# Plain and seven-product pairs put into two stretches per group, with the k, v, c, h pieces between the seven-product ones

## The chip, the cores and the metric

The kernel runs on one core of a Trainium2 chip. The core has TensorE (PE; its weight loads are listed apart as PEld), VectorE (DVE), ScalarE (ACT), GpSimd (POOL) and SyncE (SP, which here only issues DMAs), 16 DMA engines, an on-chip memory and eight PSUM banks into which PE writes. Each engine works through its own instructions in the order in which they were built. The metric is the device time of one execution in microseconds, lower is better.

## The reference

One decoder layer over 272 positions (16 learned meta tokens, then 256 tokens), model width 4096:

```
h = rmsnorm(x, norm_g);  p = h @ w_in                       # 4096 x 16384
q, k, v, g_attn, b_conv, c_conv, h_conv, z_conv = split(p)  # 2048 columns each
o = stick_breaking_attention(heads(q), heads(k), heads(v))  # 16 heads of 128
o = group_rmsnorm(o * silu(g_attn), attn_norm_g, 16)
y = b_conv * short_conv(c_conv * h_conv, conv_w)            # width 3, causal, per channel
y = group_rmsnorm(y * silu(z_conv), conv_norm_g, 16)
return rmsnorm(x + concat([o, y]) @ w_out, final_norm_g)    # meta tokens dropped
```

Attention is strictly causal: a weight is sigmoid(z) times the product of (1 - sigmoid(z)) over the keys between.

## The kernel before

**Pieces.** All weights are cut into pieces of 128 x 1024, numbered in the order of work: a list `pieces` sets the order on every engine. Each piece is loaded by SP (`raw`, a ring of 5), split into a rounded part `wh` (ACT, L314) and a remainder `wl` (DVE, L315), each in a ring of 6, and multiplied on PE with three matmuls per product (L347, L349, L350, or L339 to L341), so that the result has full precision. Loads are issued 8 pieces ahead of PE, splits 5 ahead.

**Groups.** The input projection works on 8 groups of two heads and two convolution channel groups. A group has 16 pairs of pieces for q, g, b, z over the 256 tokens (a pair is two chunks of 128 of the model width, pieces "A" and "B"), and 8 blocks of four "p" pieces for k, v, c and h over all positions (24 matmuls of 258 or 272 columns in each piece). A block is named (u, kind), u being 0 or 1 in the group and kind 0 to 3 for k, v, c, h.

**Plain and seven-product pairs.** A plain pair is a 2 x 2 block product: 8 products of three matmuls with 512 columns. A seven-product pair does it with 7 (Strassen's way, in Winograd's form): beside A and B it has two pieces "T" and "U" that are sums of weights, made by DVE (L324, L327, L328), and it takes ready-made sums of the activations (`sum`, tiles `S[j]`). It needs no product into `D22`; but as P1, P5, P6, P7 are summed apart, a group with both kinds has eight accumulators: D11, D12, D21, D22, P1, P5, P6, P7, one PSUM bank each. Group 0 has no seven-product pairs; groups 1 to 7 have seven of them (`SJ`), in turn with nine plain ones.

**Order of a group.** First all 16 pairs, then the eight blocks (32 p pieces). The accumulators lie in banks 0 to 7 during the pairs; the blocks and all small work then take banks 4 to 7 in turn. The group's attention and convolution stand beside its p pieces as "tasks", each put after a given piece: `q_t` (transposes of q), `scores`, `weights`, `trans` (transposes and block copies of the weights, `at`), `po` (the product with v), for u = 0 and 1, then `norm`, `mix` (transposes of the result, `mxh` and `mxc`, and its store to `mixd`), `conv_t` (`ct`) and `conv_out`.

**After the groups** come the output projection's four groups 8 to 11 (pairs again, six of seven products in each, in `OUT_ORDER`), 8 thin pieces, and the final norm. The attention of group 7 and its last `mix` still run beside the first pairs of group 8.

Of the kernel before, what the change touches and what calls it, by code (L numbers as in the profile page):

```python
# [61 lines left out]
def kernel(ctx, tc, xt, xin, xm, par, fg, w1, w2, out):  # L62
# [11 lines left out]
    turn = [0]  # L74
    hd = {}

    def bank(nm, i=None):

        if i is None:
            i = turn[0] % 8 if "all" in hd else 4 + turn[0] % 4  # L80
            turn[0] += 1
        return pp.tile([P, 512], F32, tag=f"b{i}", name=nm)
# [15 lines left out]
    pieces = []  # L98
    ends = {}
    fin = {}  # L100
    ms = [("m", g) for g in range(GROUPS - 1)]
    for g in range(GROUPS):
        for j in range(KC // 2):
            pieces += [(q, g, j) for q in ("ABTU" if seven(g, j) else "AB")]
            if g == 0 and 4 <= j < 13:
                pieces.append(("x", j - 4))
        fin[g] = len(pieces) - 1
        for u, b in ((0, 0), (0, 1), (1, 0), (1, 1), (0, 2), (0, 3), (1, 2), (1, 3)):
            for kc in range(4):
                pieces.append(("p", (2 * g + u, b), kc))  # L110
            ends.setdefault(g, []).append(len(pieces) - 1)
            if g == GROUPS - 1 and b == 2 + u:
                pieces += ms[2 * u:2 * u + 2]
    n1 = len(pieces)

    for g in range(GROUPS, GROUPS + 4):
        for at_, j in enumerate(OUT_ORDER):
# [7 lines left out]
    n = len(pieces)  # L125

# [9 lines left out]

    mixd = [dp.tile([P, 4, SEQ], F32, name=f"mixd{g}") for g in range(GROUPS - 1)]
# [61 lines left out]
    S = {j: sp.tile([P, 2, 4, P], F32R, name=f"sum{j}") for j in SJ}  # L199
    xr = {}  # L200
# [8 lines left out]
    def prep_x(j, parts=1):  # L209
# [41 lines left out]
    def load(i):  # L251
# [131 lines left out]
    def mm_in(i):  # L383
# [117 lines left out]
    def plain_block(u, b, e):  # L501
# [13 lines left out]
    def evict_sums(g):  # L515

        cq = wk.tile([P, 2, 512], F32, tag="cq", name=f"cq{g}")
        cb = wk.tile([P, 2, 512], F32, tag=f"cb{g % 2}", name=f"cb{g}")
        gr[g] = dict(cq=cq, cb=cb)
        if g == 0:  # L520
            return
        p1, p5, p7, p6 = (psum.pop((g, q)) for q in (P1, P5, P7, P6))
        A.copy(out=cq[:, 0], in_=p1)
        V.tensor_tensor(out=cb[:, 0], in0=p6, in1=cq[:, 0], op=ALU.add)
        V.tensor_tensor(out=cq[:, 1], in0=p7, in1=cb[:, 0], op=ALU.add)
        V.tensor_tensor(out=cb[:, 0], in0=p5, in1=cb[:, 0], op=ALU.subtract)
        V.tensor_tensor(out=cb[:, 1], in0=p5, in1=cq[:, 1], op=ALU.subtract)

    def evict(g):
        s = gr[g]  # L530
        for q, d in ((D11, s["cq"][:, 0]), (D21, s["cq"][:, 1]), (D12, s["cb"][:, 0]), (D22, s["cb"][:, 1])):
            if g:
                V.tensor_tensor(out=d, in0=psum.pop((g, q)), in1=d, op=ALU.add)
            else:
                A.copy(out=d, in_=psum.pop((g, q)))
        for c, q in (("cq", "h"), ("cb", "c")):
# [403 lines left out]
```

## Time and profile before

| what | value |
|---|---|
| time, median of 3 runs | 1828.2 us (1828.1 to 1828.71) |
| span of the profiled execution, first to last instruction | 1825.5 us |
| PE busy | 1806.8 us (99%) |
| weight loads (PEld) | 1638.5 us (90%) |
| DVE busy | 1378.6 us (76%), 2015 instructions |
| ACT busy | 1081.2 us (59%) |
| POOL busy | 111.4 us (6%) |
| DMA | 364.27 MB, mean 200 GB/s, queue of SP 59.1% of 16 engines |
| mean granted TensorE clock | 0.997 |

Matmuls are pipelined: a row's duration is longer than the distance to the next one's start, so what a matmul costs PE in a stream is read from the distance between starts. The same holds, by less, for DVE.

### The profile page before, as it was taken

Reading aid. Unit: us, or ns where it says so; the run is one execution under the profiler, and the core shown is the slowest. Engines: PE = TensorE matmul, PEld = TensorE weight load, DVE = VectorE, ACT = ScalarE, POOL = GpSimd, SP = SyncE. Lnnn points to the kernel's source line nnn. Section 1 sums busy time; section 2 is a strip of 40 time slices with the busy share of each in tenths; the row PEclk is TensorE's granted clock in tenths of the full one; section 3 lists DMA queues with packets and bytes.
Section 4 is the critical chain, followed back from the end, with each engine's and each line's share of the span. In section 5 each row is a group of like instructions: output and inputs, shape, how many; then the busy total and the mean of one; then the engine's idle time right before and its main releaser. Section 6 shows DMA issues by size and latency. Waiting matters only on the chain.

```text
span 1825.5 us, 29438 instructions
## 1 busy us (share of the span) xinstructions
PE 1806.8 (99%) x11103; PEld 1638.5 (90%) x11103; DVE 1378.6 (76%) x2015; ACT 1081.2 (59%) x1674; POOL 111.4 (6%) x172
## 2 busy tenths in 40 slices
PE   9999999999999999999999999999999999999997
PEld 7899889988998899889988998899889977888897
DVE  6686787678767866786678667866786768898986
ACT  6766556655665566556655665566556655555554
POOL 2210001000100010001000100010001031000000
PEclk9999999999999999999999999999999999999999
DMA  8865566446654665475446655655465576675655
GB/s 292 308 213 169 164 216 209 166 164 218 204 170 159 223 201 170 160 222 205 169 161 220 203 171 162 225 197 170 158 225 196 198 260 202 228 232 192 202 181 196
DMA packets 107999, 364.27 MB, mean 200 GB/s; under 512 B 12112, under 2 KB 17360, under 8 KB 107856
## 3 DMA queue, kind: packets, MB, share of 16 engines
q1 hardware_dynamic: 103824, 358.72, 59.1%
q10 hardware_dynamic: 4032, 3.67, 0.6%
q8 instruction: 87, 1.43, 0.3%
q14 instruction: 56, 0.46, 0.1%
HBM read 354.48 MB, written 7.86 MB: 198 GB/s over the span
## 4 chain that ended last, share of the span: by engine, by line
PE 97%; DVE 1%; ACT 1%; DMA 0%; issue 0%; SPq 0%; DVEq 0%; ACTq 0%
PE P L347 17%; PE P L350 17%; PE P L349 17%; PE mm L339 14%; PE mm L340 13%; PE mm L341 13%; DVE wl L315 1%; PE mo L763 0%; PE mo L762 0%; PE mo L761 0%; PE z L609 0%; PE po L655 0%; ACT wh L314 0%; DMA raw<-w 0%; DMA xr<-xt 0%
## 5 line engine op out<-in xcount | busy, mean ns | idle before, releaser
L314 ACT CAST wh<-raw 128x1024 fp32r<-128x1024 f32 (+3 forms) x721 | 692.8, 992 | 527.2 <-PE mm L340 203.4
L315 DVE TENSOR_TENSOR wl<-raw,wh 128x1024 fp32r<-128x1024 f32 (+3 forms) x721 | 815.1, 1157 | 245.9 <-ACT wh L314 236.4
L339 PE MATMUL mm<-xs,wh 128*128 128x258 f32 (+1 forms) x2048 | 589.2, 288 | 0.9 <-ACT wh L314 0.7
L340 PE MATMUL mm<-xs,wh 128*128 128x258 f32 (+1 forms) x2048 | 581.9, 284 | 0.0
L341 PE MATMUL mm<-xs,wl 128*128 128x258 f32 (+1 forms) x2048 | 581.8, 284 | 0.0
L339 PEld LDWEIGHTS mm<-xs,wh 128*128 128x128 f32 x2048 | 385.6, 188 | 4.1 <-ACT wh L314 0.9
L340 PEld LDWEIGHTS mm<-xs,wh 128*128 128x128 f32 x2048 | 385.7, 188 | 0.6
L341 PEld LDWEIGHTS mm<-xs,wl 128*128 128x128 f32 x2048 | 385.6, 188 | 0.0
L347 PE MATMUL P<-wh,xs 128*128 128x512 f32 x779 | 304.7, 391 | 1.9 <-ACT wh L314 1.9
L350 PE MATMUL P<-wl,xs 128*128 128x512 f32 x779 | 303.7, 390 | 0.0
L349 PE MATMUL P<-wh,xs 128*128 128x512 f32 x779 | 303.6, 390 | 0.0
L347 PEld LDWEIGHTS P<-wh,xs 128*128 128x128 f32 x779 | 146.6, 188 | 32.1 <-ACT wh L314 2.2
L350 PEld LDWEIGHTS P<-wl,xs 128*128 128x128 f32 x779 | 146.5, 188 | 31.4 <-DVE wl L315 0.6
L349 PEld LDWEIGHTS P<-wh,xs 128*128 128x128 f32 x779 | 146.7, 188 | 29.9
L350 PE MATMUL P<-wl,mixh 128*128 128x512 f32 (+1 forms) x392 | 148.3, 378 | 0.5 <-DVE wl L315 0.5
L347 PE MATMUL P<-wh,mixl 128*128 128x512 f32 (+1 forms) x392 | 148.6, 379 | 0.0
L349 PE MATMUL P<-wh,mixh 128*128 128x512 f32 (+1 forms) x392 | 148.2, 378 | 0.0
L324 DVE TENSOR_TENSOR t<-raw,raw 128x1024 f32<-128x1024 f32 (+1 forms) x73 | 87.6, 1200 | 24.6 <-DMA raw<-w 24.3
L314 ACT CAST wh<-t 128x1024 fp32r<-128x1024 f32 (+1 forms) x73 | 75.7, 1036 | 46.8 <-PE P L349 32.5
L315 DVE TENSOR_TENSOR wl<-t,wh 128x1024 fp32r<-128x1024 f32 (+1 forms) x73 | 87.6, 1200 | 4.2 <-ACT wh L314 3.4
L350 PEld LDWEIGHTS P<-wl,mixh 128*128 128x128 f32 x392 | 74.2, 189 | 13.1 <-DVE wl L315 1.4
L347 PEld LDWEIGHTS P<-wh,mixl 128*128 128x128 f32 x392 | 74.3, 190 | 12.0 <-ACT wh L314 0.3
(243 smaller groups left out, 1712.4 us busy)
## 6 DMA issues: line engine op xcount, KB each, us to landing
raw<-w SPq DMA_DIRECT2D x614, 512.0 KB, 4.0
raw<-w SPq DMA_DIRECT2D x32, 384.0 KB, 3.5
raw<-xin SPq DMA_DIRECT2D x8, 512.0 KB, 4.6
xr<-xt SPq DMA_DIRECT2D x15, 272.0 KB, 4.7
raw<-mixd SPq DMA_DIRECT2D x7, 512.0 KB, 3.3
res<-xin SPq DMA_DIRECT2D x12, 256.0 KB, 5.9
out<-res SPq DMA_DIRECT2D x4, 512.0 KB, 3.2
mixd<-mfh ACTq DMA_DIRECT2D x14, 128.0 KB, 2.1
```

Of the source, the lines that this page charges most:

```text
L314: nc.scalar.copy(out=h[:, c], in_=t[:, c])
L315: nc.vector.tensor_tensor(out=lo[:, c], in0=t[:, c], in1=h[:, c].bitcast(F32), op=ALU.subtract)
L324: nc.vector.tensor_tensor(out=s[:, :2 * hw].rearrange("p (a b) -> p a b", a=2), in0=a[:, :2 * hw].rearrange("p (a b) -> p a b", a=2), in1= ...
L339: nc.tensor.matmul(out=o, lhsT=h, rhs=x[:, 0, s:], start=k == 0, stop=False)
L340: nc.tensor.matmul(out=o, lhsT=h, rhs=x[:, 1, s:], start=False, stop=False)
L341: nc.tensor.matmul(out=o, lhsT=lo, rhs=x[:, 0, s:], start=False, stop=k == KC - 1)
L347: nc.tensor.matmul(out=o, lhsT=a[1], rhs=h, start=key not in begun, stop=False)
L349: nc.tensor.matmul(out=o, lhsT=a[0], rhs=h, start=False, stop=False)
L350: nc.tensor.matmul(out=o, lhsT=a[0], rhs=lo, start=False, stop=last)
```

## The change

Two things change in the groups' order and one in their make-up.

- Each of groups 1 to 6 has eleven seven-product pairs and five plain ones; group 7 has eight and eight; group 0 stays plain. That is 25 plain pairs turned into seven-product ones.
- A new function `in_pieces` writes the order. A group begins with its plain pairs, in turn with the last two blocks (c and h of u = 1) of the group before ("R"); the attention of the group before is planned into this stretch. Then come the seven-product pairs, each followed by two p pieces of the group's own first six blocks ("S"). Plain pairs first completes D22, whose bank is copied out (`open_rows`) and is from then on the one bank for all blocks and small work of the stretch: the blocks, the second head's `po`, `mix` and `conv_t` come after one another in it (`block_bank`, `spare`). The tasks `mix`, `conv_t`, `conv_out` and the second `norm` move into the next group's seven-product stretch (`slot`). Accumulators change sides from group to group. Group 7 ends with four blocks by themselves ("Z").
- Eleven sums of activations do not fit on the chip. Five stay (`HELD`); six (`LENT`) are made in group 0 (`late_sums`), written to DRAM (`lend`) and loaded again by each group that uses them, into a ring of two (`lent`), 512 KB each.

Less weighty: `evict` takes all accumulators but D22 at one place behind the last seven-product pair, and the first output group starts its seven-product pairs one place later (`OUT_FIRST`).

```diff
-SJ = (2, 4, 6, 8, 10, 12, 14)
+HELD = (1, 4, 7, 10, 13)
+LENT = (2, 5, 8, 11, 14, 15)
+SJ = tuple(j for pair in zip(LENT, HELD + (None,)) for j in pair if j is not None)
+LAST_SJ = SJ[:8]
...
+OUT_FIRST = (0, 1, 2, 3, 4, 8, 5, 9, 6, 10, 7, 11, 12, 13, 14, 15)
...
+    first = ((0, 0), (0, 1), (0, 2), (0, 3), (1, 0), (1, 1))
+    last = ((1, 2), (1, 3))
+    for g in range(GROUPS):
+        plain = [j for j in range(KC // 2) if not seven(g, j)]
+        left = blocks_of(g - 1, last) if g else []
+        for n, j in enumerate(plain):
+            pair(g, j)
...
+            take, left = (left[:1], left[1:]) if n < 4 else ([], left)
+            for t in take:
+                block(*t)
...
+        todo = blocks_of(g, first if g < GROUPS - 1 else ((0, 0), (0, 1), (1, 0), (1, 1)))
+        for j in sevens(g):
+            pair(g, j)
+            block(*todo.pop(0))
+        for t in todo:
+            block(*t)
...
+    def late_sums(j):
+        x = xs[j // 2][:, 2 * (j % 2):2 * (j % 2) + 2, :, META:L].bitcast(F32)
+        t = wk.tile([P, 2, SEQ], F32, tag="cb1", name=f"xt{j}")
+        nc.vector.tensor_tensor(out=t, in0=x[:, :, 0], in1=x[:, :, 1], op=ALU.add)
+        d = lent(j)
+        token_sums(d, t, j)
...
+        if p[0] == "A" and 0 < p[1] < GROUPS and p[2] in LENT and seven(*p[1:]):
+            S[p[2]] = lent(p[2])
+            nc.sync.dma_start(out=S[p[2]].bitcast(F32), in_=sumd[p[2]])
...
+    def block_bank(i):
+        kind, g = zone[i]
+        (u, b), d = pieces[i][1], 4 * (g % 2)
+        if kind == "R":
+            return 4 - d
+        if kind == "Z":
+            return d + 2 * ((2 * u + b) % 2)
+        return d + D22 if g else (4, 5, 6, 0, 1, 2)[{(0, 0): 0, (0, 1): 1, (0, 2): 2, (0, 3): 3, (1, 0): 4, (1, 1): 5}[u, b]]
...
-        for u, z in ((0, f + 6), (1, f + 15)):
-            later(z, scores, g, u)
-            later(z + 3, weights, g, u)
-            later(z + 5, trans, g, u)
-            later(z + 8, po, g, u)
-        later(f + 25, norm, g, "h")
-        later(f + 29 if g < GROUPS - 1 else n1 + 1, mix, g, "h")
...
+        for u, z in ((0, 5), (1, 12)):
+            later(after(f, z), scores, g, u)
+            later(after(f, z + 3), weights, g, u)
+            later(after(f, z + 5), trans, g, u)
+            later(after(f, z + 8), po, g, u)
...
+        later(after(f, 22), norm, g, "h")
+        later(after(f, 25) if end else slot(g + 1, 2), mix, g, "h")
+        later(after(e, 2) if end else slot(g + 1, 4), conv_t, (2 * g, 2 * g + 1))
+        later(after(e, 3) if end else slot(g + 1, 4) + 1, conv_out, g)
+        later(after(e, 5) if end else slot(g + 1, 5), norm, g, "c")
+        later(after(e, 8) if end else slot(g + 1, 6), mix, g, "c")
```

**DVE, one unit.** Before, on DVE in a group's pair stretch, the unit that repeats is one seven-product pair and one plain pair (number behind `wl` and `raw`: the piece; `t` the sum for T):

```order
L324 TENSOR_TENSOR t252_6274<-raw251_6215,raw252_6233 128x1024
L315 TENSOR_TENSOR wl250_6252<-raw250_6203,wh250_6251 128x1024
L315 TENSOR_TENSOR wl251_6262<-raw251_6215,wh251_6261 128x1024
L315 TENSOR_TENSOR wl252_6271<-raw252_6233,wh252_6270 128x512
L327 TENSOR_TENSOR raw251_6215<-raw251_6215,t252_6274 128x512
L315 TENSOR_TENSOR wl253_6287<-t252_6274,wh253_6286 128x1024
L328 TENSOR_TENSOR raw251_6215<-raw252_6233,raw251_6215 128x512
L315 TENSOR_TENSOR wl254_6299<-raw251_6215,wh254_6298 128x1024
L315 TENSOR_TENSOR wl255_6317<-raw255_6268,wh255_6316 128x1024
```

After, on DVE in the seven-product stretch of group 3, the unit is one seven-product pair (pieces 279 to 282) and two p pieces (here 278, and 283 of the next):

```order
L396 TENSOR_TENSOR t280_6664<-raw279_6580,raw280_6611 128x1024
L387 TENSOR_TENSOR wl278_6642<-raw278_6566,wh278_6641 128x1024
L387 TENSOR_TENSOR wl279_6652<-raw279_6580,wh279_6651 128x1024
L387 TENSOR_TENSOR wl280_6661<-raw280_6611,wh280_6660 128x512
L399 TENSOR_TENSOR raw279_6580<-raw279_6580,t280_6664 128x512
L387 TENSOR_TENSOR wl281_6677<-t280_6664,wh281_6676 128x1024
L400 TENSOR_TENSOR raw279_6580<-raw280_6611,raw279_6580 128x512
L387 TENSOR_TENSOR wl282_6689<-raw279_6580,wh282_6688 128x1024
L387 TENSOR_TENSOR wl283_6719<-raw283_6658,wh283_6718 128x1024
```

The nine instructions are the same in kind and order; pieces 250 and 255 of a plain pair have become p pieces, and eleven such units now follow each other.

**PE, one hand-over of a bank.** Before, on PE, the transposes `mxh` of group 2 stand inside a block, in a bank of their own:

```order
L339 MATMUL mm5_3_5840<-xs1_125,wh225_5653 128x258
L340 MATMUL mm5_3_5840<-xs1_125,wh225_5653 128x258
L341 MATMUL mm5_3_5840<-xs1_125,wl225_5654 128x258
L577 MATMUL mxh2_5865<-ident_93,cq2_4725 128x128 x4
L339 MATMUL mm5_3_5840<-xs2_126,wh226_5684 128x258
L340 MATMUL mm5_3_5840<-xs2_126,wh226_5684 128x258
```

After, on PE in group 3's seven-product stretch (`mm6_0`, the first block, has ended nine matmuls earlier):

```order
L419 MATMUL P0_3_5711<-wh268_6434,xs2_132 128x512
L421 MATMUL P0_3_5711<-wh268_6434,xs2_132 128x512
L422 MATMUL P0_3_5711<-wl268_6435,xs2_132 128x512
L674 MATMUL mxh2_6539<-ident_99,cq2_5571 128x128 x4
L419 MATMUL P5_3_6307<-wh269_6450,lent5_6352 128x512
L421 MATMUL P5_3_6307<-wh269_6450,lent5_6352 128x512
```

The transposes have moved behind the B piece (268) of the third seven-product pair and now write the bank that the block `mm6_0` used before them and `mm6_1` uses after them.

**SP.** Before, on SP, the loads of such a unit are pieces alone:

```order
L274 DMA raw255_6268<-w1 128x1024
L274 DMA raw256_6284<-w1 128x1024
L274 DMA raw257_6296<-w1 128x1024
L274 DMA raw258_6314<-w1 128x1024
L274 DMA raw261_6349<-w1 128x1024
```

After, on SP in group 3, the sum for the seventh seven-product pair goes out in front of the B piece of the fifth:

```order
L346 DMA raw277_6550<-w1 128x1024
L346 DMA raw278_6566<-w1 128x1024
L346 DMA raw279_6580<-w1 128x1024
L328 DMA lent11_6831<-sumd11_89 128x1024
L346 DMA raw280_6611<-w1 128x1024
```

Every second unit now has a fifth load; its place in the ring of two is freed by PE's last use of the sum two rounds earlier, and the load of piece 280 stands behind that wait.

More of the change, by code (lines that the diff above doesn't have):

```diff
@@ L50, in hwid, with sevens, in_pieces, pair @@
     return 384 if g == GROUPS + 3 else 512
+def sevens(g):
+    return OUT_SJ if g >= GROUPS else SJ if 0 < g < GROUPS - 1 else LAST_SJ if g else ()
 def seven(g, j):
-    return j in (OUT_SJ if g >= GROUPS else SJ if g else ())
+    return j in sevens(g)
+def in_pieces():
+    out, zone = [], []
+    def pair(g, j):
+        for q in "ABTU" if seven(g, j) else "AB":
+            out.append((q, g, j))
+    def block(u, b, kcs):
+        for kc in kcs:
+            out.append(("p", (u, b), kc))
+    def blocks_of(g, pairs):
+        return [(2 * g + u, b, kcs) for u, b in pairs for kcs in ((0, 1), (2, 3))]
+    first = ((0, 0), (0, 1), (0, 2), (0, 3), (1, 0), (1, 1))
[5 more added lines that the diff above has]
+            pair(g, j)
+            if g == 0 and 4 <= j < 13:
+                out.append(("x", j - 4))
+            take, left = (left[:1], left[1:]) if n < 4 else ([], left)
+            for t in take:
+                block(*t)
+        for t in left:
+            block(*t)
+        zone += [("R", g)] * (len(out) - len(zone))
+        todo = blocks_of(g, first if g < GROUPS - 1 else ((0, 0), (0, 1), (1, 0), (1, 1)))
[3 more added lines that the diff above has]
+        for t in todo:
+            block(*t)
+        zone += [("S", g)] * (len(out) - len(zone))
+    for i, t in enumerate(blocks_of(GROUPS - 1, ((0, 2), (0, 3), (1, 2), (1, 3)))):
+        block(*t)
+        if i in (1, 3, 5, 7):
+            out.append(("m", i // 2))
+    zone += [("Z", GROUPS - 1)] * (len(out) - len(zone))
+    return out, zone
 G0, CW0, AG0, CG0, NPAR = 0, 32, 80, 96, 112
@@ L74 @@
     turn = [0]
+    free = [[4, 5, 6, 7]]
     hd = {}
@@ L79, in bank @@
         if i is None:
-            i = turn[0] % 8 if "all" in hd else 4 + turn[0] % 4
+            i = free[0][turn[0] % len(free[0])]
             turn[0] += 1
@@ L92 @@
     nc.sync.dma_start(out=pt, in_=par)
-    pieces = []
-    ends = {}
-    fin = {}
+    pieces, zone = in_pieces()
+    ends, fin, top = {}, {}, {}
     ms = [("m", g) for g in range(GROUPS - 1)]
[L102 to L113, printed above, removed]
+    for i, p in enumerate(pieces):
+        if p[0] == "p":
+            ends[p[1]] = i
+        elif p[0] in "ABTU":
+            top[p[1]] = i
+        if p[0] == "p" and zone[i][0] == "S":
+            fin[p[1][0] // 2] = i
     n1 = len(pieces)
     for g in range(GROUPS, GROUPS + 4):
-        for at_, j in enumerate(OUT_ORDER):
+        for at_, j in enumerate(OUT_ORDER if g > GROUPS else OUT_FIRST):
             for q in "ABTU" if seven(g, j) else "AB":
@@ L125 @@
     n = len(pieces)
+    real = [i for i, p in enumerate(pieces) if p[0] in "ABTUpo"]
+    nth = {i: q for q, i in enumerate(real)}
     where, c1, c2 = {}, 0, 0
@@ L535, in evict @@
                 A.copy(out=d, in_=psum.pop((g, q)))
+        if not g:
+            A.copy(out=cb[:, 1], in_=psum.pop((g, D22)))
         for c, q in (("cq", "h"), ("cb", "c")):
@@ L810 @@
         plan_group(g)
+    for q, j in enumerate(LENT):
+        later(after(top[0], 4 * q + 2), late_sums, j)
+        later(after(top[0], 4 * q + 4), lend, j)
     tasks.sort(key=lambda t: t[0])
-    later(fin[0], finish_stats)
+    later(top[0], finish_stats)
+    plain_end = {g: max(i for i in range(n1) if pieces[i][0] == "B" and pieces[i][1] == g and not seven(*pieces[i][1:]))
+                 for g in range(GROUPS)}
     for i in range(1 - SPLITS, n):
@@ L825 @@
         p = pieces[i]
+        if "all" not in hd:
+            free[0] = spare(i)
         if i < n1:
@@ L829 @@
                 plain_block(*p[1], i)
-            if p[0] == ("U" if p[1] else "B") and p[2] == SJ[-1]:
-                evict_sums(p[1])
+            if i in plain_end.values():
+                open_rows(p[1])
+            if i in top.values():
+                evict(p[1])
                 if p[1] == GROUPS - 1:
                     open_mix(0)
-            if i in fin.values():
-                evict(pieces[i][1])
             if i == n1 - 1:
@@ L852 @@
             if "all" not in hd:
-                hd["all"], turn[0] = True, 0
+                hd["all"], turn[0], free[0] = True, 0, list(range(8))
             _, nb, kc = p
@@ L908 @@
         hw = hwid(GROUPS + c // 1024)
-        for j in OUT_ORDER:
+        for j in OUT_ORDER if c else OUT_FIRST:
             m1, m2 = w[2 * j], w[2 * j + 1]
```

93 lines of the change are left out of this document (55 added, 38 removed).

## Prediction

> **What bounds the kernel now.** I read the busy shares first, then the chain of waits.
>
> ```profile
> span 1825.5 us, 29438 instructions
> PE 1806.8 (99%) x11103; PEld 1638.5 (90%) x11103; DVE 1378.6 (76%) x2015; ACT 1081.2 (59%) x1674; POOL 111.4 (6%) x172
> PE 97%; DVE 1%; ACT 1%; DMA 0%; issue 0%; SPq 0%; DVEq 0%; ACTq 0%
> ```
>
> The chain that ended last lies on PE for 97% of the span, so the stream of matmuls sets the time, and what the change takes out of it counts in full as long as the other engines keep up. Shares are averages over stages, so next the busy times by stretch: the p stretch of group 0, and the pair stretch and the p stretch of one later group.
>
> ```profile
> core 0: us, PE busy (x) PEld busy (x) DVE busy (x) ACT busy (x) POOL busy (x), PEclk, DMA share, GB/s
> 85.00:202.00 117.00, 117.00 (x893) 113.26 (x892) 86.15 (x159) 73.28 (x127) 6.41 (x10) 1.00 0.56 188
> 383.80:461.00 77.20, 77.20 (x344) 63.92 (x343) 65.41 (x78) 45.49 (x60) 2.50 (x4) 1.00 0.63 204
> 461.00:565.60 104.60, 104.60 (x835) 102.95 (x834) 69.53 (x123) 62.73 (x115) 6.68 (x10) 1.00 0.54 177
> ```
>
> PE is busy throughout, at full granted clock. DVE is at 65.41 of 77.20 in the pair stretch and at 69.53 of 104.60 in the p stretch: mixing the two levels its load. Third, the waits of PE for other engines; the columns are total, times, longest.
>
> ```profile
> PE mxc L577 <- ACT cb L571: 2.8, 1, 2.8
> PE mm L339 <- DVE cb L527: 0.2, 1, 0.2
> ```
>
> There is next to nothing to win back from waits. The only larger one is at the end of the groups.
>
> **The change part by part.**
>
> *Fewer matmuls.* Distances between starts, from the timeline of PE:
>
> ```profile
> 399.30 0.39 PE L347 MATMUL P<-wh,xs 128*128 128x512 f32 x1
> 399.98 0.39 PE L347 MATMUL P<-wh,sum 128*128 128x512 f32 x1
> 461.02 0.29 PE L341 MATMUL mm<-xs,wl 128*128 128x272 f32 x1
> 461.39 0.28 PE L341 MATMUL mm<-xs,wl 128*128 128x272 f32 x1
> 559.42 0.28 PE L341 MATMUL mm<-xs,wl 128*128 128x258 f32 x1
> 559.54 0.39 PE L347 MATMUL P<-wh,xs 128*128 128x512 f32 x1
> ```
>
> Three matmuls of 512 columns lie between the first two rows (one row each at L347, L349, L350): 0.68 / 3 = 0.2267 us each. Three of 272 columns take 0.37, so 0.123 each. The last two rows show a p matmul followed by a pair's: 0.12 us, so changing over costs nothing, and the change does that twice per pair. A plain pair is 24 x 0.2267 = 5.44 us, a seven-product pair 21 x 0.2267 = 4.76, a p piece 24 x 0.123 = 2.96. 25 pairs lose three matmuls each: 75 x 0.2267 = **17.0 us off PE**. The p pieces are as many as before.
>
> *More work for DVE and ACT.* Here is one unit of the pair stretch on DVE, from one wait for U's cast to the next:
>
> ```profile
> 409.07 2.36 DVE L315 TENSOR_TENSOR wl<-raw,wh 128x1024 fp32r<-128x1024 f32 x2 [1.19 <-ACT wh L314]
> 411.35 1.22 DVE L324 TENSOR_TENSOR t<-raw,raw 128x1024 f32<-128x1024 f32 x1
> 412.48 2.96 DVE L315 TENSOR_TENSOR wl<-raw,wh 128x1024 fp32r<-128x1024 f32 x3
> 415.36 0.68 DVE L327 TENSOR_TENSOR raw<-raw,t 128x512 f32<-128x512 f32 x1
> 415.96 1.22 DVE L315 TENSOR_TENSOR wl<-t,wh 128x1024 fp32r<-128x1024 f32 x1
> 417.09 0.68 DVE L328 TENSOR_TENSOR raw<-raw,raw 128x512 f32<-128x512 f32 x1
> 418.97 2.36 DVE L315 TENSOR_TENSOR wl<-raw,wh 128x1024 fp32r<-128x1024 f32 x2 [1.20 <-ACT wh L314]
> ```
>
> The unit takes 418.97 - 409.07 = 9.90 us, 1.20 of it waiting. The new unit (one seven-product pair, two p pieces) has the same nine instructions, and PE needs 4.76 + 2 x 2.96 = 10.68 us for it. A stretch of eleven wants 11 x 9.90 = 108.9 us of DVE against 11 x 10.68 = 117.5 of PE. DVE has other work there:
>
> ```profile
> L461 DVE TENSOR_TENSOR kT<-mm,rstd 128x272 f32<-128x272 f32 x16 | 6.9, 431 | 0.0
> L471 DVE STREAM_TRANSPOSE yv<-vt 128x288 f32<-128x288 f32 x16 | 7.3, 457 | 7.8 <-ACT za L637 7.8
> L452 DVE COPY vv<-yv 32x64 f32<-32x64 f32 x128 | 23.8, 186 | 1.9
> L177 DVE TENSOR_SCALAR nc<-ssc 128x4 f32<-128x4 f32 x8 | 1.6, 202 | 0.2
> L314 ACT CAST wh<-raw 128x1024 fp32r<-128x1024 f32 x612 | 626.2, 1049 | 483.0 <-PE mm L340 190.8 <-DVE raw L328 172.0 <-PE P L349 56.9
> ```
>
> Two k blocks at 0.43; one v block (0.43 by its likeness to k, 0.46, 8 x 0.19); one c, one h and the reading of `po` (seven more of 0.43 as an estimate from the k row); 22 small operations of two norms at up to 0.20: about 0.9 + 2.4 + 3.0 + 4.4 = 10.7. So DVE is about level with PE (119.6 against 117.5, plus the two p pieces at the end of the stretch, 5.9 for PE and 2 x 1.18 for DVE). It can also use the 1.20 us waits for these operations, which would take up to 13 us off. And it starts ahead: the tightest ring place is free when A begins, and its next piece is wanted a unit's rest later (1.36 + 0.68 + 1.36 + 1.36 + 2.96 = 7.7), while cast and remainder take 1.05 + 1.18. **Cost taken: 0**; the cover is that lead of some 4.4 us, when another cast of 1.05 stands before it, and its loss is the first rival below. ACT gets 25 x (1.05 + 0.55) = 40 us more and is at 59%: hidden.
>
> *One bank for many.* Three times a group (before `mxh`, `ct` and `mxc`) a block ends, PE does A and B (nine matmuls, 2.04 us), and within these DVE must have read the block: one operation in front of it (1.18) and the read (0.43) fit with 0.4 to spare. The other hand-overs have twelve matmuls (2.72) or are read by ACT. The nearest row is the second wait quoted above, in which a block's first matmul waited for DVE to have read an accumulator's bank: 0.2 us, once. Ends: 0, as PE met no such wait anywhere else, and 0.7 for each, when one more 512-column DVE operation (0.68) stands ahead. With 21 of them (groups 1 to 7): 0 to 14.7 us; a gain is excluded because the change only adds such waits. I take 0.2 each, nearer that row: **+4.2**.
>
> *Moved attention.* It has now 8 p pieces and 5 plain pairs beside it. For u = 1 before:
>
> ```profile
> 508.24 0.25 PE z L608 x2
> 525.25 2.23 ACT L454 COPY at<-ya 32x96 f32<-32x96 f32 x8
> 531.91 0.22 PE po L651 x2
> ```
>
> From `z` to the last copy of the weights are 527.48 - 508.24 = 19.2 us; `po` then stood 4.4 us behind, with nothing waiting. After, between `z` and `po` stand two plain pairs, two p pieces, A and B, and the first head's `po` (ten matmuls, some 1.1): 2 x 5.44 + 2 x 2.96 + 2.04 + 1.1 = 19.9. So it fits with 0.7 to spare: **0**, ends 0 and 7 x (2 x 1.18 - 0.7) = 11.6, if two of DVE's wide operations more hold the copies back.
>
> *Sums made, stored, reloaded.* In group 0 six sums more:
>
> ```profile
> L232 POOL TENSOR_TENSOR sf<-xr 128x128 f32<-128x128 f32 x7 | 5.8, 830 | 62.0 <-ACT xr L217 36.4 <-DVE xr L215 25.6
> raw<-w SPq DMA_DIRECT2D x614, 512.0 KB, 4.0
> ```
>
> DVE has two operations of about 0.68 each for a sum, 8.2 us, against 30.9 idle in group 0's p stretch; POOL's four of at most 0.83 come to 20 at most, in a stretch where it is busy 6.41 of 117. The reloads take 40 loads of 512 KB on SP, like a piece (4.0 us to landing). A unit in the present pair stretch loads four pieces of 0.524 MB in 4.76 + 5.44 = 10.2 us, which the window has as 204 GB/s at a DMA share of 0.63; the new unit, with a sum in every second one, loads 4.5 in 10.68: 221 GB/s, a share of about 0.68. Hidden: **0**. In SP's queue the sum waits for PE's last use of its place and the B piece of that pair stands behind; half a unit of the lead covers it, else DVE's `t` comes up to 1.5 us late.
>
> *The end of the groups.* The large wait:
>
> ```profile
> 1489.55 0.39 PE L350 MATMUL P<-wl,mixh 128*128 128x512 f32 x1
> 1492.71 1.46 PE L577 MATMUL mxc<-ident,cb 128*128 128x128 f32 x4 [2.77 <-ACT cb L571]
> 1493.82 0.78 PE L347 MATMUL P<-wh,mixl 128*128 128x512 f32 x1
> 1499.04 0.40 PE L347 MATMUL P<-wh,mixl 128*128 128x512 f32 x1
> 1494.00:1500.00 6.00, 6.00 (x18) 4.71 (x18) 3.08 (x4) 1.57 (x4) 0.00 (x0) 0.59 0.80 302
> ```
>
> The last `mix` waits 2.77 us for the norm, and then twelve matmuls take 5.22 us in place of 12 x 0.2267 = 2.72, at a granted clock of 0.59: with 0.6 for slow transposes, 5.9 us in all. After the change the same chain follows the last block by about as many pairs. **0**; ends -5.9 (wait gone) and +6 (a second such wait, for `mxh`, which is put earlier against the norm).
>
> [...]
>
> Sum against the profiled execution: 1825.5 - 17.0 + 4.2 = 1812.7. The median of the runs is 1828.2, 2.7 above that span: **1815.4, said as 1815**.
>
> **The rivals.**
>
> 1. *DVE becomes the bound in the seven-product stretches* (slower). With the 10.7 us spread over eleven units and T's sum 0.9 late by the sum's load, a unit takes 9.90 + 0.97 + 0.9 = 11.77, if none of DVE's waits are filled. Over PE's 10.68 that is 12.0 a group, less the lead of 4.4: 7.6, in six groups 46. Time: 1828.2 - 17.0 + 46 = 1857. It decides from a unit of 10.68 + (4.4 + 17.0 / 6) / 11 = 11.3 us. For it speaks that sum; against it that DVE is idle 15% of the present pair stretch and that its norms fit in the waits. Chance 0.08.
> 2. *Each hand-over is late by one wide DVE operation and more*, about 1 us, when DVE's lead is used up and it takes its order literally. 21 us: 1828.2 - 17.0 + 21 = 1832. It decides from 17.0 / 21 = 0.8 us each. For it: 0.4 us of room. Against: PE's list of waits shows one such case among 64 blocks. Chance 0.11.
> 3. *The hand-overs stop PE so often that the clock falls each time.* If each cost the 0.2 us and the 2.5 us of slow matmuls seen at the end of the groups, 21 x 2.7 = 57: 1828.2 - 17.0 + 57 = 1868. Against it: 0.2 us is far from 2.8, and the three stretches shown stand at 1.00. Chance 0.03. [...]
> 4. *All is hidden and the last wait goes too*: 1828.2 - 17.0 - 5.9 = 1805. It needs the norm of group 7 to be done 2.8 us earlier against PE; nothing in the change shortens its chain. Chance 0.13.
>
> **How the numbers follow.** The forecast (1815; its own bounds 1811 with the hand-overs at 0 and 1826 with them at 14.7) has 0.65; the rivals as above. The range from 1805 to 1828 takes in rival 4 below; above, it leaves out rivals 1 and 3 and most of rival 2 (its milder part, some 0.03, lies inside): 0.19. A difference of 0.2% (3.7 us) is about what a measurement of this kernel can tell from none. Faster than 1824.5: the forecast all but 0.02 and rival 4: 0.76. Slower than 1831.9: rivals 1 and 3 and a good third of rival 2: 0.15. Between: 0.09.
>
> **What would show it.** Right: PE's instructions 75 fewer among those of 512 columns; PE waits for DVE or ACT in the new stretches together of some 4 us, at `mxh`, `ct`, `mxc`; DVE's unit at 10.7 us, with PE the engine that ends last; one wait of some 3 us around `mxc` of group 7. Wrong, and how: waits of PE for `wl` (L387) that grow along a stretch mean rival 1; waits at L674 or at a block's first matmul (L411) above 0.8 us mean rival 2; a granted clock below 1.00 inside groups 1 to 7 means rival 3; waits of `po` mean that the attention's cover of 20 us was cut too fine; PE waiting for `lent` means that the reloads are late, which the sum takes as hidden.

## The result, and the profile after

The changed kernel takes 1845.4 us (median of 4 runs, 1842.5 to 1850.7) against 1828.15 beside it (1827.6 to 1828.7): ratio 1.0096, 95% interval 1.0074 to 1.0118. It is slower by 1%; the forecast was 0.7% faster. The profiled execution took 1842.7 us. Here and below one execution of the kernel before (1977.2 us) and one of tail_late (8597.0 us) are left out, as they lie far outside all others. From its page (span; busy time by engine; the chain that ended last, by engine):

```profile
span 1840.8 us, 29653 instructions
PE 1793.8 (97%) x11028; PEld 1621.1 (88%) x11028; DVE 1502.7 (82%) x2150; ACT 1124.2 (61%) x1735; POOL 143.2 (8%) x188
PE 86%; DVE 5%; issue 3%; ACT 2%; DMA 2%; POOL 2%; SPq 0%; DVEq 0%; POOLq 0%; ACTq 0%
```

The 75 matmuls are gone (11103 to 11028) and PE is busy 13.0 us less, yet the span has grown by 15.3: PE stands still more. The chain, 97% PE before, now passes through DVE, ACT and DMA for some 9%. What PE waits for (total, times, longest), the same view as before:

```profile
PE mxc L674 <- DVE cc L575: 12.9, 6, 2.4
PE ct L762 <- DVE cy L588: 6.6, 1, 6.6
PE mxh L674 <- DVE kT L553: 5.2, 6, 1.3
PE P L419 <- ACT wh L386: 2.8, 3, 1.7
PE mxc L674 <- DVE kT L553: 2.1, 1, 2.1
PE P L422 <- DVE wl L387: 1.8, 4, 0.6
```

Three of these rows are the transposes that now share one bank with the blocks, waiting for DVE to have read a block (`kT`, `cc`) out of it; `ct` at L588 is the end of the groups. The waits for casts (`wh`) and remainders (`wl`) shown here lie at the very start and behind the groups. By stretch, the seven-product stretch of group 3 and the plain stretch behind it:

```profile
core 0: us, PE busy (x) PEld busy (x) DVE busy (x) ACT busy (x) POOL busy (x), PEclk, DMA share, GB/s
592.00:707.00 115.00, 112.37 (x730) 102.88 (x730) 98.22 (x133) 68.25 (x102) 2.54 (x5) 1.00 0.66 214
707.00:775.00 68.00, 68.00 (x439) 61.95 (x439) 54.55 (x89) 46.22 (x80) 9.97 (x9) 1.00 0.57 192
```

The plain stretch with the attention has no idle PE at all. All of this group's loss lies in its seven-product stretch.

Adding up, over PE's timeline, by how much each start lies later than the usual distance behind the matmul before it gives 24.7 us before and 56.9 after. The difference, 32.2 us, less the 17.0 of the matmuls, gives the span's 15.3 to a tenth. Of it, 24.5 stand in front of `mxh` (6.4), `mxc` (16.6) and `ct` (1.5) in groups 1 to 7, and 7.9 after 1425 us, at the end of the groups (16.9 against 9.0).

**One hand-over, row by row.** In group 5, block c of the first head ends on PE when the A piece begins; then come A, B and `mxc`:

```profile
1020.78 0.40 PE L419 MATMUL P<-wh,xs 128*128 128x512 f32 x1
1024.78 0.63 PE L674 MATMUL mxc<-ident,cb 128*128 128x128 f32 x4 [1.78 <-DVE cc L575]
```

DVE and, below it, ACT in the same microseconds:

```profile
1019.09 0.69 DVE L400 TENSOR_TENSOR raw<-raw,raw 128x512 f32<-128x512 f32 x1
1019.69 0.16 DVE L665 TENSOR_TENSOR ssc<-nc,fac 128x4 f32<-128x4 f32 x1
1020.95 1.23 DVE L387 TENSOR_TENSOR wl<-raw,wh 128x1024 fp32r<-128x1024 f32 x1 [1.11 <-ACT wh L386]
1023.07 1.22 DVE L387 TENSOR_TENSOR wl<-raw,wh 128x1024 fp32r<-128x1024 f32 x1 [0.89 <-ACT wh L386]
1024.21 0.42 DVE L575 TENSOR_TENSOR cc<-mm,rstd 128x258 f32<-128x258 f32 x1
```

```profile
1019.87 1.06 ACT L386 CAST wh<-raw 128x1024 fp32r<-128x1024 f32 x1 [5.09 <-DVE ssc L665]
1020.83 1.27 ACT L668 ACTIVATE cb<-cb,ssc 128x128 f32<-128x128 f32 x4
1022.01 1.98 ACT L386 CAST wh<-raw 128x1024 fp32r<-128x1024 f32 x2
```

The read of c takes 0.42 us, but begins 3.4 us behind the block's end: in DVE's order stand two remainders before it, each waiting for its cast on ACT. The first cast is that of the U piece. Its wait of 5.09 us is for U's sum of weights (L400, which ended at 1019.78): the view names the norm's last operation (`ssc`), which ended 0.07 later. The second cast stands behind the norm's scaling (`cb`, 1.27 us). PE needs 2.04 us for A and B, and stops. Over the groups the reads of k ahead of `mxh` begin 2.2 to 3.0 us behind their block, those of c ahead of `mxc` 3.4 to 4.1, in groups 1 to 6. Before the change DVE stood waiting for PE at about half of the reads of v and c. The groups of these reads, kernel before (L467, L483), then changed kernel (L559, L575); the last column is DVE's idle time ahead of them and what ended it:

```profile
L467 DVE TENSOR_TENSOR vt<-mm,rstd 128x272 f32<-128x272 f32 x16 | 7.0, 437 | 8.5 <-PE mm L341 8.5
L483 DVE TENSOR_TENSOR cc<-mm,rstd 128x258 f32<-128x258 f32 x16 | 6.8, 424 | 4.8 <-PE mm L341 4.8
```

```profile
L559 DVE TENSOR_TENSOR vt<-mm,rstd 128x272 f32<-128x272 f32 x16 | 7.0, 434 | 2.0 <-PE mm L413 1.9
L575 DVE TENSOR_TENSOR cc<-mm,rstd 128x258 f32<-128x258 f32 x16 | 6.5, 407 | 0.0
```

Same operation, same duration; the slack in front of it has gone.

But late reads are not new. In the kernel before, DVE had no idle time ahead of the reads of k (0.0, the row of L461 in the prediction), and in groups 1 to 6 the first c block was read 3.56 us behind its end. Here in group 2, first the start of the next block on PE, then the read:

```profile
523.18 0.28 PE L339 MATMUL mm<-xs,wh 128*128 128x258 f32 x1
526.74 0.42 DVE L483 TENSOR_TENSOR cc<-mm,rstd 128x258 f32<-128x258 f32 x1
```

PE went on without a wait, as its next block went into another bank. The changed kernel's reads of c (3.4 to 4.1 us) are hardly later; it is the next user that now wants the same bank.

**The end of the groups.** PE's wait, and DVE in the ten microseconds before it:

```profile
1489.59 0.69 PE L762 MATMUL ct<-ident,cy 128*128 128x128 f32 x2 [6.56 <-DVE cy L588]
```

```profile
1478.94 1.83 DVE L544 COPY at<-ya 32x96 f32<-32x96 f32 x8
1482.20 0.42 DVE L580 TENSOR_TENSOR cc<-mm,cc 128x258 f32<-128x258 f32 x1
1488.86 0.67 DVE L588 SCALAR_TENSOR_TENSOR cy<-cc,pt,cy 128x256 f32<-128x256 f32 x1
```

Group 7 has only 16 p pieces left at its end, so the second head's weights (`at`) and the last convolution (`cc`, `cy`) come to DVE one right behind the other, and `ct` comes before the convolution is done. Between the convolution's steps DVE has remainders and sums for the output projection to make, too.

### The profile page after: what moved, and what is told of

It is laid out like the page before. It is cut to its first block, busy times and chain, and to the rows that moved or that the text cites. A ratio compares the mean times of both kernels' runs of the same rounds, so it can differ in the third digit from the quotient of the medians.

```text
span 1840.8 us, 29653 instructions
## 1 busy us (share of the span) xinstructions
PE 1793.8 (97%) x11028; PEld 1621.1 (88%) x11028; DVE 1502.7 (82%) x2150; ACT 1124.2 (61%) x1735; POOL 143.2 (8%) x188
## 4 chain that ended last, share of the span: by engine, by line
PE 86%; DVE 5%; issue 3%; ACT 2%; DMA 2%; POOL 2%; SPq 0%; DVEq 0%; POOLq 0%; ACTq 0%
PE P L419 16%; PE P L422 16%; PE P L421 16%; PE mm L413 11%; PE mm L412 11%; PE mm L411 11%; DVE wl L387 2%; DMA raw<-w 1%; ACT wh L386 1%; DMA raw<-mixd 1%; PE mo L868 0%; PE mo L867 0%; PE mo L866 0%; PE z L706 0%; DVE raw L400 0%
## 5 line engine op out<-in xcount | busy, mean ns | idle before, releaser
L386 ACT CAST wh<-raw 128x1024 fp32r<-128x1024 f32 (+2 forms) x746 | 710.3, 980 | 499.9 <-DVE raw L400 160.8
L387 DVE TENSOR_TENSOR wl<-raw,wh 128x1024 fp32r<-128x1024 f32 (+2 forms) x746 | 837.1, 1149 | 174.9 <-ACT wh L386 171.1
L419 PE MATMUL P<-wh,xs 128*128 128x512 f32 x654 | 259.5, 397 | 1.7 <-ACT wh L386 1.7
L422 PE MATMUL P<-wl,xs 128*128 128x512 f32 x654 | 255.1, 390 | 0.3 <-DVE wl L387 0.2
L421 PE MATMUL P<-wh,xs 128*128 128x512 f32 x654 | 254.9, 390 | 0.0
L396 DVE TENSOR_TENSOR t<-raw,raw 128x1024 f32<-128x1024 f32 (+1 forms) x98 | 118.2, 1206 | 35.1 <-DMA raw<-w 33.1
L422 PEld LDWEIGHTS P<-wl,xs 128*128 128x128 f32 x654 | 122.7, 188 | 27.2 <-DVE wl L387 1.1
L419 PEld LDWEIGHTS P<-wh,xs 128*128 128x128 f32 x654 | 123.0, 188 | 24.5 <-ACT wh L386 1.9
L421 PEld LDWEIGHTS P<-wh,xs 128*128 128x128 f32 x654 | 122.9, 188 | 21.8
L386 ACT CAST wh<-t 128x1024 fp32r<-128x1024 f32 (+1 forms) x98 | 101.7, 1038 | 45.5 <-PE P L421 14.5
L387 DVE TENSOR_TENSOR wl<-t,wh 128x1024 fp32r<-128x1024 f32 (+1 forms) x98 | 117.9, 1203 | 4.8 <-ACT wh L386 4.7
```

Source lines behind the costliest of these rows:

```text
L386: nc.scalar.copy(out=h[:, c], in_=t[:, c])
L387: nc.vector.tensor_tensor(out=lo[:, c], in0=t[:, c], in1=h[:, c].bitcast(F32), op=ALU.subtract)
L396: nc.vector.tensor_tensor(out=s[:, :2 * hw].rearrange("p (a b) -> p a b", a=2), in0=a[:, :2 * hw].rearrange("p (a b) -> p a b", a=2), in1= ...
L419: nc.tensor.matmul(out=o, lhsT=a[1], rhs=h, start=key not in begun, stop=False)
L421: nc.tensor.matmul(out=o, lhsT=a[0], rhs=h, start=False, stop=False)
L422: nc.tensor.matmul(out=o, lhsT=a[0], rhs=lo, start=False, stop=last)
```

## The experiments

The theories: A, a block's read is late because of what stands ahead of it in DVE's order; B, DVE simply has more work than PE in the stretch; C, the reloaded sums hold up the queue of loads. For the end of the groups, T1 to T3. Medians stand against 1845.4 (changed) and about 1828 (before, measured beside each).

**Later transposes (t_slot).**

```diff
-        return pieces.index(("B", g, sevens(g)[c]))
+        return pieces.index(("T", g, sevens(g)[c]))
```

> The transposes mxh, ct and mxc stand behind the T piece in place of the B piece: 15 matmuls (3.4 us) instead of 9 (2.04 us) between a block's end and them, and 6 (1.36 us) instead of 12 before the next block uses the bank. Changed kernel: PE waits 5.2 us for mxh and 15.0 for mxc over seven groups, median 1845 us. Theory A (DVE reads the block 1.0 to 2.3 us too late, because the read stands in DVE's order behind remainders for pieces further ahead): the wait for mxh goes below 1 us, that for mxc to about 6 (7 x 0.9), waits at the next block for ACT below 2; about 14 us less, 1831. Theory B (DVE has more work in the stretch than PE, so PE must wait somewhere): the waits move to remainders (wl), the time stays within 4 us of 1845. Theory C (the loads of the sums hold up the pieces): as B.

Median 1834.4 us (1832.1 to 1837.0), ratio to the kernel before 1.0032 (1.002 to 1.0044). PE's waits:

```profile
PE mm L411 <- ACT cy L764: 11.8, 7, 2.6
PE ct L762 <- DVE cy L588: 6.4, 1, 6.4
PE mm L411 <- ACT mfc L685: 0.7, 4, 0.2
```

The waits for `mxh` and `mxc` are gone altogether, and no remainder is waited for instead (1.7 us in all, 2.0 in the changed kernel): against B. The other side of the hand-over was too short at one place in each group: the block behind `ct` waits for ACT, whose reading of `ct` stood behind its copies of v's blocks (2.9 us in group 5). Not foreseen, and the reason for 1834 in place of 1831.

**Without the reloads (no_lent).**

```diff
-            S[p[2]] = lent(p[2])
-            nc.sync.dma_start(out=S[p[2]].bitcast(F32), in_=sumd[p[2]])
+            S[p[2]] = S[HELD[0]]
```

> The 40 reloads of sums are left out; the pairs that used them multiply one of the resident sums instead (other numbers, the same matmuls). Theory A (DVE's order) and theory B (DVE's amount of work): nothing changes, 1845 us within 4, waits for mxh and mxc within 20% of 5.2 and 15.0 us. Theory C (the loads in SP's queue delay the B pieces, these DVE's sums, and these its reads of the blocks): both waits fall by half or more, 10 to 20 us less, 1825 to 1835.

Median 1840.9 us (1840.2 to 1846.9; the changed kernel 1842.5 to 1850.7).

```profile
PE mxc L673 <- DVE cc L574: 10.8, 6, 2.4
PE mxh L673 <- DVE kT L552: 5.1, 6, 1.0
```

`mxh` waits as before, `mxc` 12.8 in place of 15.0 (with the row of 2.0 for `kT`). The reloads cost between nothing and 5 us (4.5 at the medians, with ranges that overlap); C is not the cause.

**mxc one block later (mxc_slot8).**

```diff
-else slot(g + 1, 6), mix, g, "c")
+else slot(g + 1, 8 if g < GROUPS - 2 else 6), mix, g, "c")
```

> The transposes mxc alone stand one block later (behind the ninth seven-product pair instead of the seventh, groups 1 to 6), so that the norm on DVE and its scaling on ACT lie a block ahead of the read that they wait for. Theory A1 (of the 2.3 us at mxc some 1.3 come from the norm: its small operations on DVE and the scaling on ACT stand ahead of the casts and remainders in front of the read): the wait for mxc falls from 2.1 to 2.6 us each to about 1.0 in six groups, 8 us less, about 1837. Rival A2 (a block's read comes that late there by DVE's remainders alone): the wait stays above 1.8 us each and the time within 3 us of 1845.

Median 1851.4 us (1845.8 to 1853.6): 6 us more, though the ranges overlap. The wait has clearly grown:

```profile
PE mxc L674 <- DVE cc L580: 17.6, 6, 3.6
```

Neither theory has this: A1 expected shorter waits, A2 the same time. The read of h, now the one in front, begins 3.7 to 5.2 us behind its block (1.8 to 2.9 in the changed kernel in groups 2 to 6, where PE had stopped a block earlier). So a stop of PE ahead of the block had let DVE catch up; without it DVE is later at the next. In mxc_R below, where nothing stops PE there, h is read 3.1 to 4.3 us behind as well.

**Without the norm's operations on DVE (no_norm).** In `norm`:

```diff
-        V.tensor_scalar(out=ss, ...); r = rsqrt_raw(ss, ...); V.tensor_tensor(out=ss, ...)
+        if q == "h" or g == GROUPS - 1:
+            V.tensor_scalar(out=ss, ...); r = rsqrt_raw(ss, ...); V.tensor_tensor(out=ss, ...)
```

> In the changed kernel's order, the eleven small DVE operations of the convolution's norm are left out in groups 0 to 6 (its scaling on ACT then uses the plain sum of squares and does not wait for DVE; other numbers). The read of c, ahead of mxc, started 3.4 to 4.1 us behind its block's end; that of k, ahead of mxh, 2.2 to 3.0. Theory A1 (the norm holds DVE and ACT back by the difference, and with DVE and PE level there nothing makes it up within a block): c's read comes 2 to 2.7 us behind, the waits for mxc fall from 15.0 us to 7, and the median by 8, to 1837. Rival A2 (c's read is late by the remainders alone): both within 20%, the median within 3 us of 1845.

Median 1833.8 us (1831.1 to 1837.3), 11.6 less.

```profile
PE mxc L675 <- DVE cc L575: 6.2, 6, 1.7
PE mxh L675 <- DVE kT L553: 4.4, 6, 0.8
```

c's read comes 2.2 to 3.4 us behind, and `mxc` waits 6.5 in place of 15.0. Eleven operations of under 0.2 us, and the scaling that waits for them, make the difference between `mxh` and `mxc`. That fits A, with a share of B: DVE has so little to spare that 2 us of small work aren't made good within a block.

**Only mxh and mxc later (hc_T), `ct` behind B.**

```diff
-... slot(g + 1, 2), mix, g, "h")
-... slot(g + 1, 6), mix, g, "c")
+... slot(g + 1, 2, "T"), mix, g, "h")
+... slot(g + 1, 6, "T"), mix, g, "c")
```

> mxh and mxc alone stand behind the T piece; ct stays behind the B piece. With all three behind T, PE waited 11.8 us for ACT to read ct (seven times 1.3 to 2.6 us) and not at all for mxh and mxc; with ct behind B, the changed kernel had waited 0.9 us for it. Theory A (a read of the bank is late by what stands ahead of it in its engine's order, so each hand-over wants the longer side where the later reader is): the waits for mxh, mxc and ct together fall below 4 us, the median goes from 1834.4 (all three behind T) to about 1825, level with the kernel before or 0.2% faster. Theory B (DVE has more work than PE there): the time won shows up as waits for remainders and the median stays above 1831.

Median 1836.6 us (1833.3 to 1839.8), no better than with all three behind T.

```profile
PE mxc L674 <- DVE cc L575: 5.7, 6, 1.0
PE mm L411 <- ACT mfc L685: 5.5, 6, 0.9
```

Without the stop at `ct`, c's read is again 3.7 to 4.0 us late, more than the 3.4 that T allows; and `mxc`, late itself, leaves ACT too little time ahead of the next block. A wait taken away in this stretch came back one place on, as with mxc_slot8.

**The convolution later in group 7 (tail_late); the attention earlier (tail_early).**

```diff
# tail_late: conv_t, conv_out, norm c, mix c at e + 5, 6, 8, 11 in place of 2, 3, 5, 8
# tail_early:
-        for u, z in ((0, 5), (1, 12)):
+        for u, z in ((0, 3), (1, 9)) if end else ((0, 5), (1, 12)):
```

> Group 7 alone: its conv_t, conv_out, second norm and second mix stand three pieces later beside group 8. In the changed kernel PE waits 6.6 us there for DVE's convolution, followed by half the granted clock. Theory T1 (the convolution stands on DVE behind the weights of the second head's attention, which in group 7 have moved next to it; PE comes too early): the wait goes below 1.5 us and the slow clock behind it goes, 7 to 10 us less, about 1837. Rival T2 (DVE is 7 us behind there with all its work, so PE waits for the next remainder instead): the time stays within 3 us of 1845 and a new wait of 4 us or more stands in the next 20 us.

> Group 7 alone: both heads' attention begins two and three pieces earlier, with the convolution where it was. Putting the convolution and the second mix later had only moved the wait (from ct, 6.6 us, to mxh and mxc, 4.7 us). Theory T3 (in group 7 the weights of the second head's attention and the convolution come to DVE and ACT in the same ten microseconds; apart, neither is late): the wait at ct falls from 6.6 us below 1.5, no new one above 1.5 stands in the next 40 us, and the median falls by 6 to 9 us, to about 1837. Rival T2 (DVE and ACT are behind there by their amount of work): waits of together 4 us or more remain between group 7's last block and the end of mxh and mxc, the median above 1841.

Medians 1842.8 (1841.8 to 1844.9) and 1844.0 us (1842.0 to 1845.2): within 3 us of the changed kernel, which its own range of 8 us doesn't tell from nothing. PE's waits in the tail, first of tail_late:

```profile
PE mxc L674 <- issue: 2.4, 1, 2.4
PE mxh L674 <- ACT cq L668: 2.1, 2, 1.8
```

then of tail_early:

```profile
PE mxh L674 <- ACT cq L668: 2.3, 2, 2.0
PE ct L762 <- DVE cy L588: 0.3, 1, 0.3
```

The wait at `ct` goes either way, as T1 and T3 had it, and smaller ones come up where a norm's scaling is late: 4.5 us in two places in tail_late, where ACT scales for `mxc` only at 1514.55 us and the transposes begin at 1515, and 2.3 in tail_early. Neither brought the 6 to 10 us expected. The late starts after 1425 us fall from 16.9 to 12.6 us with the earlier attention; the time doesn't show it, since in that profile half-clock stretches behind stops at `mxc` came in four groups, where the changed kernel's profile has one (three more at 1.7 us each; see the end). One of them shows a granted clock of 0.76 from 1209 to 1216 us, and the mean over that profile is 0.993 against 0.996.

**Both together (hc_T_tail).**

> Both edits together: mxh and mxc behind T, group 7's attention earlier. Under theories A and T3 the gains add: about 1817 (1825 less 8), which is 0.6% faster than the kernel before. Under the rivals: above 1828.

Median 1834.0 us (1833.2 to 1837.8), ratio 1.0037 (1.0024 to 1.005). As the first half had gained 9 us and not 20, this could not reach 1817.

**mxc out of the stretch (mxc_R), and with the tail (mxc_R_tail).** `mxh` behind T, and:

```diff
+        far = g < GROUPS - 2
-        later(... slot(g + 1, 5), norm, g, "c")
-        later(... slot(g + 1, 6), mix, g, "c")
+        later(... after(fin[g + 1], 2) if far else slot(g + 1, 5), norm, g, "c")
+        later(... after(fin[g + 1], 7) if far else slot(g + 1, 6, "T"), mix, g, "c")
# mxc_R_tail besides: group 7's attention as in tail_early, its norm h at f + 19 in place of 22
```

> mxh behind T, ct behind B as in the changed kernel; the convolution's norm and mxc of groups 0 to 5 leave the seven-product stretch and stand in the plain stretch that follows it (2 and 7 pieces in), where three banks are spare. Theory A1 (the norm's small operations and its scaling, in a stretch in which DVE is level with PE, make the reads of a bank late, and whatever takes the bank there waits): waits for mxh, ct, mxc and the blocks behind them fall together from about 24 us to below 5, no half clock before 1480 us, median about 1822, 0.3% faster than the kernel before. Rival B (DVE's amount of work is too much, with the plain stretch full too): waits for remainders appear in the plain stretch or for po, median above 1830.

> As the one before, and in group 7 the attention begins two and three pieces earlier and the first norm stands three pieces earlier, six pieces ahead of its mix. The earlier attention alone took the wait at ct from 6.6 to 0.3 us and left 2.3 at mxh for the norm's scaling. Theory T3 (each of these waits has its own late predecessor): the waits in the tail fall to below 3 us, median 4 to 6 us below the kernel without this edit, about 1817, 0.6% faster than before. Rival T2 (ACT and DVE are behind there by their amount of work): another wait of 2 us or more comes up, the same median within 2 us.

Medians 1822.6 us (ratio 0.997, 0.9958 to 0.9982) and 1820.0 us (0.9948, 0.9934 to 0.9962): both faster than the kernel before. Of mxc_R's waits these are left at the transposes, the first of them in the tail:

```profile
PE ct L762 <- DVE cy L588: 6.8, 1, 6.8
PE ct L762 <- DVE vt L559: 1.4, 2, 0.7
PE mxc L674 <- DVE kT L553: 0.6, 1, 0.6
```

c's read still begins 3.9 to 4.3 us behind its block, though no norm stands near it. It does no harm, because nothing takes the bank before the next block, 21 matmuls or 4.76 us on. So the norm is not needed for the lateness: with PE not stopping, DVE is about 4 us late there in any case, and the hand-over decides whether that costs. In mxc_R_tail's tail one wait at the transposes is left (`mxc`, 4.5 us, with half the granted clock for 6.8 us behind it), which is more than T3 allowed.

**ACT reads the blocks (act_read).** For k, v and c, the changed kernel's order untouched:

```diff
-        V.tensor_tensor(out=kt, in0=src, in1=rstd, op=ALU.mult)
+        A.copy(out=kt, in_=src)
+        V.tensor_tensor(out=kt, in0=kt, in1=rstd, op=ALU.mult)
```

> The changed kernel's order, with the blocks of k, v and c read out of their bank by ACT (a copy; DVE multiplies afterwards, from the on-chip memory). With DVE reading, k came 2.2 to 3.0 us and c 3.4 to 4.1 us behind the block's end. Theory A (what makes the read late is DVE's queue, level with PE and with remainders in front; ACT has some 38% idle and stands no further ahead than its ring allows): ACT reads within 1.5 us of the block's end, waits for mxh and mxc fall together from 20 us to below 5, median about 1826. Rival D (ACT is tied to DVE, since it waits 3 to 5 us each unit for DVE's sum for U, and comes as late): the waits stay above 12 us together, median above 1838.

Median 1821.1 us (1819.4 to 1823.1), ratio 0.9966 (0.9953 to 0.9979): 24 us less than the changed kernel, though DVE has as many operations as before and ACT 48 more. The same hand-over of group 5, PE and then ACT:

```profile
1005.74 0.40 PE L419 MATMUL P<-wh,xs 128*128 128x512 f32 x1
1008.26 0.63 PE L677 MATMUL mxc<-ident,cb 128*128 128x128 f32 x4 [0.31 <-ACT cc L577]
```

```profile
1007.76 0.36 ACT L577 COPY cc<-mm 128x258 f32<-128x258 f32 x1
```

The reads of c begin 2.0 to 2.4 us behind the block, more than theory A's 1.5 (k's 1.1), and the six waits for `mxc` come to 2.3 us:

```profile
PE ct L765 <- DVE cy L591: 7.2, 1, 7.2
PE mxc L677 <- ACT cc L577: 2.3, 6, 0.6
```

This decides it: the place of the read in its engine's order was the cause of the stops, not the amount of DVE's work (B), which is the same, nor ACT's tie to DVE (D). That DVE has little to spare (its remainders end 2.1 to 2.5 us ahead of PE at the least) is taken as the condition for it; no run shows that apart.

**The best two (best2, best3).** best2 is mxc_R_tail with group 7's last `mix` at e + 11; best3 is act_read with the three edits of the tail.

> The kernel with mxc in the plain stretch and group 7's attention earlier (1820.0 us), with group 7's last mix three pieces later. There PE had waited 4.7 us at mxc, with half the granted clock for 6.8 us behind it. Theory T3 (a late predecessor, not too much work): the wait goes below 1 us and the slow clock with it, median 4 to 7 us lower, about 1815. Rival T2: 2 us or more of new waits come up within 20 us, median within 2 us of 1820.

> ACT reads k, v and c; in group 7 the attention begins two and three pieces earlier, the first norm stands three pieces earlier and the last mix three later; all else as in the changed kernel. If the two losses are apart (the hand-overs 24 us, the tail 6 to 8 us), the median is that of the kernel with ACT reading (1821.1) less 5 to 7 us: about 1815, PE's waits between 60 and 1480 us together below 5 us. If the tail's waits follow from how far ahead PE is when it gets there (PE comes sooner, DVE does not), a new wait of 4 us or more stands in the tail and the median stays within 2 us of 1821.

1817.5 us (ratio 0.9946, 0.9934 to 0.9959) and 1817.3 us (0.9945, 0.9931 to 0.9959). The earlier attention and norm had brought mxc_R 2.6 us, and all three edits of the tail bring act_read 3.8. The later `mix` alone, in best2, shows 2.5 at the medians; by the ratios (0.9948 without it, 0.9946 with it) that can't be told from nothing. All are less than expected, since part of a wait removed came back. First a row of best2, then two of best3:

```profile
PE P L419 <- DVE mixl L690: 4.1, 2, 2.1
```

```profile
PE P L419 <- DVE mixl L693: 2.6, 1, 2.6
PE ct L765 <- DVE cy L591: 2.4, 1, 2.4
```

All lie in the tail. Hand-overs and tail are thus two losses. Of the first, 3.4 us of waits for `mxc` are left in best3; of the second, some 4 of 8 us are won. best3 has PE busy 1790.3 us, 16.5 less than the kernel before.

## Why the prediction was wrong, by its steps

- **Fewer matmuls, -17.0: right.** 75 fewer, at unchanged distances (0.227 us); where PE no longer stops (best3), its busy time is 16.5 us lower.
- **More work for DVE, 0: right as a sum, wrong in what it was checked against.** Remainders make PE wait 2.0 us in all, 0.2 of it in groups 1 to 7; rival 1 didn't come. DVE's lead, from a remainder's end to its first use on PE, worked out for each piece from the two timelines, falls from some 12.8 us in the plain stretch to 4.8 at the start of the seven-product stretch and to 2.1 to 2.5 at its lowest. The estimate of 4.4 us fits the start of the stretch and is about twice the lowest. But the lead was asked only whether a remainder comes in time. A read of a block stands in DVE's order behind the remainders of the five pieces that follow the block; with the lead down to a few microseconds, part of them is still to be done when the block ends (two in the rows above), and the read waits for them.
- **One bank for many, +4.2: the step that failed.** It measured 24.5 us, 1.17 for each of 21 hand-overs (about 0.9 at `mxh`, 2.4 at `mxc`, 0.2 at `ct`). The 0.2 us came from PE's waits in a kernel that gives each block another bank. There a late read need not make PE wait, so PE's waits don't show how late the reads are. DVE's own rows do: 3.56 us behind the block's end at the first c of groups 1 to 6, against 1.6 us that the prediction counted for one operation and the read. The profile before had this row, and the prediction didn't use it; the slack that v and c had (8.5 and 4.8 us) went besides. The step's upper end, 0.7 for each, came from one more wide operation in front; the trace shows two remainders and a cast chain. The prediction's second rival had the mechanism ("takes its order literally"), 1 us each and 1832 us, at a chance of 0.11.
- **Moved attention, 0: right.** No wait for `po` in the changed kernel.
- **Sums made, stored, reloaded, 0: nearly right.** 0 to 5 us by no_lent.
- **The end of the groups, 0, ends -5.9 and +6: outside its ends, +7.9.** The chain of the norm was looked at, and the wait at `mxc` did go; what came was `ct` behind the second head's attention, which the shortened group 7 had pushed beside the convolution. The earlier attention of tail_early took that wait to 0.3 us. The prediction named nothing there as late next.
- **Rival 3 (the clock)** was right in kind and small: in the profiled run one half-clock stretch in groups 1 to 7 (0.51 over 3.50 us, below).

Together: 24.5 - 4.2 at the hand-overs and 7.9 at the end are 28.2 us; the profiled execution lies 27.3 above the forecast of 1815.4, the rest being differences of a microsecond, up and down; the median lies 30.0 above it. In the kernel before, a block's next user had another bank; the change gives that up for one bank, and the runs show what the rotation had hidden: a first c read 3.56 us behind its block without a wait before, 2.4 us of wait at `mxc` after. The prediction didn't weigh it.

## What to carry to other kernels

When several users share one bank, price each hand-over by where its read stands in the reader's queue, not by how long the read takes (here 0.42 us, begun 3.4 us late): count what the reader has been given ahead, and read from the reader's own rows how far behind the block's end it begins. The writer's waits didn't show it here while the banks rotated (3.56 us late, no wait). Give the read to the engine with room (here ACT, 24 us), or leave more time before the next user of the bank (here 4.8 us in place of 2.0 behind c, which brought 23 us together with the later `mxh`). Where the reader has as little lead as here, expect a stop removed at one place to come back at the next: it did in mxc_slot8 (17.6 us at `mxc` after 12.9) and hc_T (5.5 us at the blocks behind), until the reader changed or the window grew.

## What the runs showed of the hardware

A stop of PE of some 2 us was followed by half the granted clock in some cases. The changed kernel at its first `mxc` (a stop of 2.09 us in the waits, a clock of 0.51 behind it), by windows: during the stop, and behind it.

```profile
290.70:292.00 1.30, 0.03 (x1) 0.06 (x1) 1.30 (x3) 1.30 (x2) 0.00 (x0) 1.00 0.84 331
292.00:295.50 3.50, 3.50 (x11) 2.86 (x12) 3.50 (x4) 1.76 (x5) 0.00 (x0) 0.51 0.84 214
```

Matmuls of 512 columns lie 0.43 us apart there (0.227 elsewhere), and at 0.51 the 3.50 us of the second window cost 1.7 us. In the profiles of the two kernels, past the first 60 us, nine starts of PE came 1.9 to 3.3 us late. Two of them were followed by such a stretch: this one (2.25 us late) and `mxc` at the end of the groups in the kernel before (2.93 us late, 0.59 from 1494 to 1500 us). Seven, 1.95 to 2.57 us late, were not. The one start later still, 6.73 us late at `ct` in the changed kernel, was (0.55 from 1489.6 to 1494 us). Of those less late, 1.51 us at most, none was. In tail_late a start at `mxh` that came 1.95 us late had matmuls 0.43 us apart behind it. So the price of a 2 us stop varies. That this makes the spread of the changed kernel's runs (8 us, against 4 with ACT reading) is not shown: tail_early, at a mean clock of 0.993 in its profiled run, spreads by 3 us.
